# Jensen-Shannon divergence on one core: products by plain fp16 multiply, their sums on TensorE, first pieces through the hardware queue

## Chip, core and metric

The kernel runs on 1 core of a Trainium2 chip. The metric is the device time of one execution in microseconds, the median of three runs. One execution is also taken by the profiler; its rows are what this document reads.

## What is computed

`p` and `q` are 1024 x 4096 in fp32. For every row one number comes out, half the sum of two divergences from the mean of the two rows:

```python
m = 0.5 * (p + q)
kl_pm = np.sum(p * np.log(p / (m + 1e-8) + 1e-8), axis=-1)
kl_qm = np.sum(q * np.log(q / (m + 1e-8) + 1e-8), axis=-1)
return (0.5 * (kl_pm + kl_qm)).astype(np.float32)
```

The kernel takes the quotients apart: it sums `p ln p + q ln q` and subtracts `(p + q) ln m`. The factor `SHIFT` inside the logarithms cancels out between the two.

## The kernel before

The 1024 rows are 8 row groups `g` of 128 partitions. A row group's 4096 columns are cut into pieces of 2048 columns, the first group into 1024, 1024, 2048: 17 pieces in all. For each piece:

- Two DMAs on GpSimd's software queue (lines 75, 76) bring `p` and `q` into one fp16 tile `pq`, of twice the piece's width. The DMA casts from fp32.
- The sum `p + q` is `sps`. For the first three pieces VectorE adds (line 81, `DVE_ADD`), for the others TensorE multiplies blocks of 512 columns by an identity `ident` and adds the two in PSUM (lines 88 and 95).
- ScalarE takes the logarithm of all of `pq` into `ab` (line 105, up to 4096 elements) and of `sps` into `c` (line 114).
- VectorE multiplies `pq` by `ab` and sums along the row in one instruction (line 134, `tensor_tensor_reduce`, which the profile calls CUSTOM_DVE_ANT_0), and does the same with `sps` and `c` (line 144). In the three pieces of `ACT_RED` (8, 11 and 14) it only multiplies (line 123), and ScalarE sums with a `Copy` activation (line 126).

The partial sums are columns of `dacc`; at the end of a row group VectorE adds them into a column of `res` (line 156), and at the very end SyncE stores `res` (line 163). Every engine works through its own instructions in order and waits for the others by semaphores; the framework sets the order of the instructions and when a buffer of a pool is free. `pq` and `ab` have 8 buffers each, `sps` has 2 of 2048 fp32 columns in PSUM. The loads run ahead as far as buffers and the software queue's eight semaphores allow.

Of the kernel before, what the change touches and what calls it, by code (L numbers as in the profile page):

```python
# [1 line left out]

# [5 lines left out]

SHIFT = 6634.0
MMN = 512


@with_exitstack
def kernel(
    ctx: ExitStack,
    tc: tile.TileContext,
    p: bass.AP,  # L20
    q: bass.AP,
    out: bass.AP,
):
    nc = tc.nc
    P = nc.NUM_PARTITIONS

    n_rows, n_cols = p.shape
    assert q.shape == (n_rows, n_cols)
    assert n_rows % P == 0
    n_rg = n_rows // P  # L30

    fp32 = mybir.dt.float32
    fp16 = mybir.dt.float16

    pv = p.rearrange("(p g) d -> g p d", g=n_rg)
    qv = q.rearrange("(p g) d -> g p d", g=n_rg)
    ov = out.rearrange("(p g) -> p g", g=n_rg)

    W = 2048
    assert n_cols == 4096  # L40
    widths = {0: [1024, 1024, 2048]}
    default_w = [W] * (n_cols // W)
    max_terms = 2 * max(len(widths.get(g, default_w)) for g in range(n_rg))

    big = ctx.enter_context(tc.tile_pool(name="big", bufs=8))
    mid = ctx.enter_context(tc.tile_pool(name="mid", bufs=8))
    small = ctx.enter_context(tc.tile_pool(name="small", bufs=1))
    accp = ctx.enter_context(tc.tile_pool(name="accp", bufs=6))
    psp = ctx.enter_context(tc.tile_pool(name="psp", bufs=2, space=bass.MemoryType.PSUM))

    tiny_t = small.tile([P, 1], fp32, tag="tiny")
    nc.vector.memset(tiny_t, 1e-30)  # L52
    epsc_t = small.tile([P, 1], fp32, tag="epsc")
    nc.vector.memset(epsc_t, SHIFT * 1e-8)
    res = small.tile([P, n_rg], fp32, tag="res")
    ident = small.tile([P, P], fp16, tag="ident")
    make_identity(nc, ident)

    nchunks = sum(len(widths.get(g, default_w)) for g in range(n_rg))
    DVE_ADD = {0, 1, 2}  # L60
    ACT_RED = {8, 11, 14}
    idx = 0

    for g in range(n_rg):
        ws = widths.get(g, default_w)
        nt = 2 * len(ws)
        dacc = accp.tile([P, max_terms], fp32, tag="dacc")
        col = 0
        for ci, w in enumerate(ws):
            csl = slice(col, col + w)  # L70
            col += w
            pq = big.tile([P, 2 * w], fp16, tag="pq")
            p0 = pq[:, :w]
            p1 = pq[:, w : 2 * w]
            nc.gpsimd.dma_start(out=p0, in_=pv[g, :, csl])  # L75
            nc.gpsimd.dma_start(out=p1, in_=qv[g, :, csl])  # L76
            pqf = pq[:, : 2 * w]

            if idx in DVE_ADD:
                sps = mid.tile([P, w], fp16, tag="s")  # L80
                nc.vector.tensor_tensor(  # L81
                    out=sps, in0=p0, in1=p1, op=mybir.AluOpType.add
                )
            else:
                sps = psp.tile([P, w], fp32, tag="sps")
                for k in range(w // MMN):
                    blk = slice(k * MMN, (k + 1) * MMN)
                    nc.tensor.matmul(  # L88
                        out=sps[:, blk],
                        lhsT=ident,  # L90
                        rhs=p0[:, blk],
                        start=True,
                        stop=False,
                    )
                    nc.tensor.matmul(  # L95
                        out=sps[:, blk],
                        lhsT=ident,
                        rhs=p1[:, blk],
                        start=False,
                        stop=True,  # L100
                    )

            ab = big.tile([P, 2 * w], fp16, tag="ab")
            abf = ab[:, : 2 * w]
            nc.scalar.activation(  # L105
                out=abf,
                in_=pqf,
                func=mybir.ActivationFunctionType.Ln,
                bias=tiny_t,
                scale=SHIFT,  # L110
            )

            c = mid.tile([P, w], fp16, tag="c")
            nc.scalar.activation(  # L114
                out=c,
                in_=sps,
                func=mybir.ActivationFunctionType.Ln,
                bias=epsc_t,
                scale=SHIFT * 0.5,
            )  # L120

            if idx in ACT_RED:
                nc.vector.tensor_tensor(  # L123
                    out=abf, in0=pqf, in1=abf, op=mybir.AluOpType.mult
                )
                nc.scalar.activation(  # L126
                    out=abf,
                    in_=abf,
                    func=mybir.ActivationFunctionType.Copy,
                    scale=0.5,  # L130
                    accum_out=dacc[:, 2 * ci : 2 * ci + 1],
                )
            else:
                nc.vector.tensor_tensor_reduce(  # L134
                    out=abf,
                    in0=pqf,
                    in1=abf,
                    scale=0.5,
                    scalar=0.0,
                    op0=mybir.AluOpType.mult,  # L140
                    op1=mybir.AluOpType.add,
                    accum_out=dacc[:, 2 * ci : 2 * ci + 1],
                )
            nc.vector.tensor_tensor_reduce(  # L144
                out=c,
                in0=sps,
                in1=c,
                scale=-0.5,
                scalar=0.0,
                op0=mybir.AluOpType.mult,  # L150
                op1=mybir.AluOpType.add,
                accum_out=dacc[:, 2 * ci + 1 : 2 * ci + 2],
            )
            idx += 1

        nc.vector.tensor_reduce(  # L156
            out=res[:, g : g + 1],
            in_=dacc[:, :nt],
            axis=mybir.AxisListType.X,
            op=mybir.AluOpType.add,  # L160
        )

    nc.sync.dma_start(out=ov, in_=res)


# [1 line left out]
_INS = ['p', 'q']  # L167
_OUTS = [((1024,), 'float32')]


# [23 lines left out]
```

## Time and profile before

| What | Before |
|---|---|
| time, median of 3 runs (lowest to highest) | 118.71 us (118.48 to 118.87) |
| span of the profiled execution | 117.0 us |
| VectorE busy | 102.2 us |
| ScalarE busy | 100.2 us |
| TensorE busy with matmuls, mean granted clock | 44.5 us, 0.719 of full |
| GpSimd busy (issuing loads) | 18.8 us |
| DMA busy | from about 3 to 83 us |

The span runs from the first to the last instruction of the profiled execution; the time of a run also holds what lies around it, here 1.7 us more at the median. An engine's busy time is an average over the span. The order of events, and so what the time hangs on, is read from the chain of waits and from each engine's timeline.

### The profile page before, as it was taken

Reading aid. Unit: us, or ns where it says so; the run is one execution under the profiler, and the core shown is the slowest. Engines: PE = TensorE matmul, PEld = TensorE weight load, DVE = VectorE, ACT = ScalarE, POOL = GpSimd, SP = SyncE. Lnnn points to the kernel's source line nnn. Section 1 sums busy time; section 2 is a strip of 40 time slices with the busy share of each in tenths; the row PEclk is TensorE's granted clock in tenths of the full one; section 3 lists DMA queues with packets and bytes.
Section 4 is the critical chain, followed back from the end, with each engine's and each line's share of the span. In section 5 each row is a group of like instructions: output and inputs, shape, how many; then the busy total and the mean of one; then the engine's idle time right before and its main releaser. Section 6 shows DMA issues by size and latency. Waiting matters only on the chain.

```text
span 117.0 us, 477 instructions
## 1 busy us (share of the span) xinstructions
PE 44.5 (38%) x112; PEld 14.8 (13%) x112; DVE 102.2 (87%) x78; ACT 100.2 (86%) x41; POOL 18.8 (16%) x40
## 2 busy tenths in 40 slices
PE   0000001952065381908367900394064393029000
PEld 0000000320021120303021300131021131002000
DVE  0023999989999999999999999999999799996991
ACT  0039976999999999999999999999999999998600
POOL 6943111131111311113211100000000000000000
PEclk9999999999755555555555587559958769955555
DMA  2999999999999999999999999999300000000000
GB/s 10 166 157 206 218 209 220 209 217 209 218 209 217 211 214 213 213 216 211 214 211 216 210 218 207 218 209 220 71 6 0 0 0 0 0 0 0 0 0 1
DMA packets 5042, 16.81 MB, mean 144 GB/s; under 512 B 688, under 2 KB 688, under 8 KB 5040
## 3 DMA queue, kind: packets, MB, share of 16 engines
q0 software_dynamic: 4896, 16.78, 72.8%
q1 hardware_dynamic: 144, 0.00, 0.1%
q8 instruction: 1, 0.02, 0.1%
q14 instruction: 1, 0.01, 0.0%
HBM read 33.55 MB, written 0.00 MB: 287 GB/s over the span
## 4 chain that ended last, share of the span: by engine, by line
ACT 62%; issue 13%; DMA 13%; DVE 6%; POOL 4%; POOLq 0%; ACTq 0%
ACT ab L105 34%; ACT c L114 21%; DMA pq<-in_q_dram 13%; ACT ab L126 8%; DVE ab L134 4%; DVE c L144 2%; POOL pq L75 2%; POOL pq L76 1%; POOL ident masks.py:199 0%; POOL ident masks.py:197 0%; DVE res L156 0%; POOLq masks.py:199 0%; DVE dacc L144 0%; ACTq L105 0%; POOLq L178 0%
## 5 line engine op out<-in xcount | busy, mean ns | idle before, releaser
L105 ACT ACTIVATE ab<-pq,tiny_t 128x4096 f16<-128x4096 f16 (+1 forms) x17 | 59.4, 3513 | 1.9 <-DMA pq<-in_q_dram 1.9
L134 DVE CUSTOM_DVE_ANT_0 ab<-pq,ab 128x4096 f16<-128x4096 f16 (+1 forms) x14 | 57.5, 4115 | 1.7 <-ACT ab L105 1.6
L88 PE MATMUL sps<-pq,ident 128*128 128x512 f16 x56 | 32.0, 571 | 60.4 <-DVE dacc L144 42.4
L144 DVE CUSTOM_DVE_ANT_0 c<-sps,c 128x2048 f16<-128x2048 f32 (+2 forms) x17 | 36.5, 2159 | 0.8 <-ACT c L114 0.8
L95 PE MATMUL sps<-pq,ident 128*128 128x512 f16 x56 | 31.8, 568 | 3.2 <-DMA pq<-in_q_dram 3.2
L114 ACT ACTIVATE c<-sps,epsc_t 128x2048 f16<-128x2048 f32 (+2 forms) x17 | 31.6, 1874 | 0.3 <-PE sps L95 0.3
L95 PEld LDWEIGHTS <-ident 128*128 128x128 f16 x56 | 7.3, 130 | 71.7 <-issue 70.6
L75 POOL DMA_DIRECT2D pq<-in_p_dram x17 | 9.3, 546 | 25.0 <-DMA pq<-in_p_dram 15.9
L76 POOL DMA_DIRECT2D pq<-in_q_dram x17 | 9.1, 538 | 21.1 <-DMA pq<-in_q_dram 21.1
L126 ACT ACTIVATE ab<-ab 128x4096 f16<-128x4096 f16 x3 | 10.9, 3635 | 0.0
L81 DVE TENSOR_TENSOR sps<-pq 128x1024 f16<-128x1024 f16 (+1 forms) x3 | 2.6, 867 | 9.1 <-DMA pq<-in_q_dram 9.1
L88 PEld LDWEIGHTS <-ident 128*128 128x128 f16 x56 | 7.5, 134 | 20.7 <-issue 15.8
L105 ACT ACT_TABLE_LOAD x1 | 1.3, 1283 | 7.6 <-DMA pq<-in_q_dram 7.6
L123 DVE TENSOR_TENSOR ab<-pq,ab 128x4096 f16<-128x4096 f16 x3 | 6.9, 2285 | 0.0
L144 DVE DVE_READ_ACCUMULATOR2_ANT dacc<- 128x1 f32 x17 | 1.4, 82 | 0.0
L156 DVE TENSOR_REDUCE res<-dacc 128x1 f32<-128x4 f32 (+1 forms) x8 | 1.2, 152 | 0.0
L134 DVE DVE_READ_ACCUMULATOR2_ANT dacc<- 128x1 f32 x14 | 1.1, 82 | 0.0
L52 DVE MEMSET tiny_t<- 128x1 f32 x1 | 0.1, 59 | 0.8 <-PEq L178 0.8
L126 ACT ACTIVATION_READ_ACCUMULATOR ab<-ab 128x1 f32 x3 | 0.7, 221 | 0.0
masks.py:199 POOL TENSOR_SCALAR_AFFINE_SELECT ident<-ident 128x128 f16<-128x128 f16 x1 | 0.3, 307 | 0.1
masks.py:197 POOL MEMSET ident<- 128x128 f16 x1 | 0.2, 205 | 0.3 <-POOLq L178 0.3
L178 POOL MEMSET const-float32-0.0<- 128x1 f32 x1 | 0.1, 99 | 0.2 <-issue 0.2
(4 smaller groups left out, 0.4 us busy)
## 6 DMA issues: line engine op xcount, KB each, us to landing
pq<-in_p_dram POOLq DMA_DIRECT2D x15, 512.0 KB, 19.1
pq<-in_q_dram POOLq DMA_DIRECT2D x15, 512.0 KB, 19.4
pq<-in_p_dram POOLq DMA_DIRECT2D x2, 256.0 KB, 5.1
pq<-in_q_dram POOLq DMA_DIRECT2D x2, 256.0 KB, 6.3
out_dram<-res SPq DMA_DIRECT2D x1, 4.0 KB, 1.4
```

Of the source, the lines that this page charges most:

```text
L75: nc.gpsimd.dma_start(out=p0, in_=pv[g, :, csl])
L76: nc.gpsimd.dma_start(out=p1, in_=qv[g, :, csl])
L81: nc.vector.tensor_tensor(out=sps, in0=p0, in1=p1, op=mybir.AluOpType.add)
L88: nc.tensor.matmul(out=sps[:, blk], lhsT=ident, rhs=p0[:, blk], start=True, stop=False,)
L95: nc.tensor.matmul(out=sps[:, blk], lhsT=ident, rhs=p1[:, blk], start=False, stop=True,)
L105: nc.scalar.activation(out=abf, in_=pqf, func=mybir.ActivationFunctionType.Ln, bias=tiny_t, scale=SHIFT,)
L114: nc.scalar.activation(out=c, in_=sps, func=mybir.ActivationFunctionType.Ln, bias=epsc_t, scale=SHIFT * 0.5,)
L123: nc.vector.tensor_tensor(out=abf, in0=pqf, in1=abf, op=mybir.AluOpType.mult)
L126: nc.scalar.activation(out=abf, in_=abf, func=mybir.ActivationFunctionType.Copy, scale=0.5, accum_out=dacc[:, 2 * ci : 2 * ci + 1],)
L134: nc.vector.tensor_tensor_reduce(out=abf, in0=pqf, in1=abf, scale=0.5, scalar=0.0, op0=mybir.AluOpType.mult, op1=mybir.AluOpType.add, accu ...
L144: nc.vector.tensor_tensor_reduce(out=c, in0=sps, in1=c, scale=-0.5, scalar=0.0, op0=mybir.AluOpType.mult, op1=mybir.AluOpType.add, accum_o ...
L156: nc.vector.tensor_reduce(out=res[:, g : g + 1], in_=dacc[:, :nt], axis=mybir.AxisListType.X, op=mybir.AluOpType.add,)
```

## The change

- **Pieces.** Row group 0 is cut into 256, 768, 1024 and 2048 columns, the last group into 2048, 1024, 768 and 256, the others stay at two times 2048: 20 pieces, numbered 0 to 19.
- **First loads.** Pieces 0 and 1 come as fp32 through SyncE's hardware queue (lines 76, 77), the others as before through GpSimd's, now lines 80 and 81. Their sums `s` are added by VectorE in fp32 (line 144).
- **Logarithms.** `ab` is as before (line 163). The sum is now in PSUM tiles `s` of 1024 columns, three buffers, so `c` is taken in halves (line 173). A one-element logarithm on constants stands at the start (line 63). There is no `Copy` activation any more.
- **Products of p and q.** For pieces of at least 1024 columns, VectorE only multiplies (line 165). TensorE sums: it multiplies blocks of 512 columns of `ab` by `half`, an identity times 0.5, and adds all of a row group's blocks up in one 512-column PSUM tile `acc` (line 108). VectorE reduces `acc` to one column (line 116). These matmuls are written behind the sums of the following piece. Smaller pieces keep the multiplying and summing instruction (line 167).
- **Products of the mean** keep it too, in halves (line 176).

The core of the diff:

```diff
-    DVE_ADD = {0, 1, 2}
-    ACT_RED = {8, 11, 14}
+    widths = {0: [256, 768, 1024, 2048], n_rg - 1: [2048, 1024, 768, 256]}
+    HW = 2
-    mid = ctx.enter_context(tc.tile_pool(name="mid", bufs=8))
+    mid = ctx.enter_context(tc.tile_pool(name="mid", bufs=4))
-    psp = ctx.enter_context(tc.tile_pool(name="psp", bufs=2, space=bass.MemoryType.PSUM))
+    psp = ctx.enter_context(tc.tile_pool(name="psp", bufs=3, space=bass.MemoryType.PSUM))
+    psa = ctx.enter_context(tc.tile_pool(name="psa", bufs=2, space=bass.MemoryType.PSUM))
+        if i < HW:
+            t = small.tile([P, 2 * w], fp32, tag=f"pq32_{i}")
+            nc.sync.dma_start(out=t[:, :w], in_=pv[g, :, csl])
+            nc.sync.dma_start(out=t[:, w : 2 * w], in_=qv[g, :, csl])
+    def reduce_on_pe(i, ab):
+        n = 2 * w // MMN
+        for k in range(n):
+            nc.tensor.matmul(
+                out=acc,
+                lhsT=half,
+                rhs=ab[:, k * MMN : (k + 1) * MMN],
+                start=(i == ones[0] and k == 0),
+                stop=(i == ones[-1] and k == n - 1),
+            )
+        if i == ones[-1]:
+            nc.vector.tensor_reduce(
+                out=slot(g), in_=acc, axis=mybir.AxisListType.X, op=Alu.add
+            )
+        if on_pe:
+            nc.vector.tensor_tensor(out=ab, in0=pq, in1=ab, op=Alu.mult)
+        else:
+            nc.vector.tensor_tensor_reduce(
+                out=ab, in0=pq, in1=ab, scale=0.5, scalar=0.0,
+                op0=Alu.mult, op1=Alu.add, accum_out=slot(g),
+            )
+        for o, n, s in sums:
+            c = mid.tile([P, SW], fp16, tag="c")
+            nc.scalar.activation(
+                out=c[:, :n], in_=s[:, :n], func=Act.Ln, bias=epsc_t, scale=SHIFT * 0.5
+            )
```

Below is how instructions stand in a row on an engine, before and after. The names are those of the tiles above; `t` is the new name of `pq`.

ScalarE in the middle of the program, before, around one `Copy` activation:

```order
L105 ACTIVATE ab<-pq,tiny_t 128x4096 [waits DMASW3_49,DMASW2_49]
L114 ACTIVATE c<-sps,epsc_t 128x2048 [waits PE_49]
L126 ACTIVATE ab,dacc<-ab 128x4096 [waits DVE_49]
L114 ACTIVATE c<-sps,epsc_t 128x2048 [waits PE_49]
L105 ACTIVATE ab<-pq,tiny_t 128x4096 [waits DMASW5_49,DMASW4_49]
```

and after:

```order
L173 ACTIVATE c<-s,epsc_t 128x1024 [waits DVE_49,PE_49] x2
L163 ACTIVATE ab<-t,tiny_t 128x4096 [waits DMASW3_49,DMASW2_49]
L173 ACTIVATE c<-s,epsc_t 128x1024 [waits DVE_49,PE_49] x2
L163 ACTIVATE ab<-t,tiny_t 128x4096 [waits DMASW5_49,DMASW4_49]
L173 ACTIVATE c<-s,epsc_t 128x1024 [waits DVE_49,PE_49] x2
```

The activation on `ab` that waited for VectorE is gone; one logarithm of 4096 and two of 1024 alternate.

VectorE in the middle of the program, before, where two products follow each other and a plain multiply comes in between:

```order
L134 ISA ab,dacc<-pq,ab 128x4096 [waits DMASW5_49,DMASW4_49,Activation_49]
L134 ISA dacc 128x1
L156 TENSOR_REDUCE res<-dacc 128x1 [waits DVE_49,Activation_49]
L144 ISA c,dacc<-sps,c 128x2048 [waits Activation_49]
L144 ISA dacc 128x1
L144 ISA c,dacc<-sps,c 128x2048 [waits Activation_49]
L144 ISA dacc 128x1
L123 TENSOR_TENSOR ab<-pq,ab 128x4096 [waits DMASW7_49,DMASW6_49]
```

and after, the whole of one row group's second piece with what follows:

```order
L165 TENSOR_TENSOR ab<-t,ab 128x4096 [waits DMASW3_49,DMASW2_49,Activation_49]
L176 ISA c,dacc<-s,c 128x1024 [waits Activation_49]
L176 ISA dacc 128x1
L176 ISA c,dacc<-s,c 128x1024 [waits Activation_49]
L176 ISA dacc 128x1
L116 TENSOR_REDUCE dacc<-acc 128x1 [waits PE_49]
L165 TENSOR_TENSOR ab<-t,ab 128x4096 [waits DMASW5_49,DMASW4_49,Activation_49]
```

The plain multiply now stands in every full piece; the product with the mean comes in two halves, and the reduction of TensorE's sum once in a row group.

VectorE at the end of the program, after:

```order
L167 ISA ab,dacc<-t,ab 128x1536 [waits DMASW1_49,DMASW0_49,Activation_49]
L167 ISA dacc 128x1
L176 ISA c,dacc<-s,c 128x768 [waits Activation_49]
L176 ISA dacc 128x1
L116 TENSOR_REDUCE dacc<-acc 128x1 [waits PE_49]
L167 ISA ab,dacc<-t,ab 128x512 [waits DMASW3_49,DMASW2_49,Activation_49]
L167 ISA dacc 128x1
L176 ISA c,dacc<-s,c 128x256 [waits Activation_49]
L176 ISA dacc 128x1
L122 TENSOR_REDUCE res<-dacc 128x1 [waits DVE_49]
```

Before, the end was one 4096-element product, one of 2048 and the reduction.

## Rows read from the trace of the kernel before

**Rows 1.** The page, busy time, share of the span and instructions of each engine.

```profile
PE 44.5 (38%) x112; PEld 14.8 (13%) x112; DVE 102.2 (87%) x78; ACT 100.2 (86%) x41; POOL 18.8 (16%) x40
```

**Rows 2.** The page, chain that ended last: shares of the span by engine.

```profile
ACT 62%; issue 13%; DMA 13%; DVE 6%; POOL 4%; POOLq 0%; ACTq 0%
```

**Rows 3.** ScalarE's timeline: start, length (us), line, operation, out<-in, count [idle before].

```profile
10.82 1.13 ACT L114 ACTIVATE c<-sps,epsc_t 128x1024 f16<-128x1024 f16 x1
11.86 1.99 ACT L105 ACTIVATE ab<-pq,tiny_t 128x2048 f16<-128x2048 f16 x1
13.75 1.13 ACT L114 ACTIVATE c<-sps,epsc_t 128x1024 f16<-128x1024 f16 x1
15.62 3.71 ACT L105 ACTIVATE ab<-pq,tiny_t 128x4096 f16<-128x4096 f16 x1 [0.74 <-DMA pq<-in_q_dram]
20.52 3.71 ACT L105 ACTIVATE ab<-pq,tiny_t 128x4096 f16<-128x4096 f16 x1 [1.19 <-DMA pq<-in_q_dram]
...
53.27 3.71 ACT L105 ACTIVATE ab<-pq,tiny_t 128x4096 f16<-128x4096 f16 x1
56.87 1.97 ACT L114 ACTIVATE c<-sps,epsc_t 128x2048 f16<-128x2048 f32 x1
58.72 7.31 ACT L105 ACTIVATE ab<-pq,tiny_t 128x4096 f16<-128x4096 f16 x2
```

**Rows 4.** VectorE's timeline, an early stretch and the end.

```profile
13.53 1.22 DVE L144 CUSTOM_DVE_ANT_0 c<-sps,c 128x1024 f16<-128x1024 f16 x1
...
14.67 2.29 DVE L134 CUSTOM_DVE_ANT_0 ab<-pq,ab 128x2048 f16<-128x2048 f16 x1
...
95.62 2.28 DVE L123 TENSOR_TENSOR ab<-pq,ab 128x4096 f16<-128x4096 f16 x1
97.82 4.42 DVE L134 CUSTOM_DVE_ANT_0 ab<-pq,ab 128x4096 f16<-128x4096 f16 x1
...
102.17 2.29 DVE L144 CUSTOM_DVE_ANT_0 c<-sps,c 128x2048 f16<-128x2048 f32 x1
...
107.84 4.43 DVE L134 CUSTOM_DVE_ANT_0 ab<-pq,ab 128x4096 f16<-128x4096 f16 x1 [1.10 <-ACT ab L105]
...
112.19 2.29 DVE L144 CUSTOM_DVE_ANT_0 c<-sps,c 128x2048 f16<-128x2048 f32 x1
...
114.52 0.16 DVE L156 TENSOR_REDUCE res<-dacc 128x1 f32<-128x4 f32 x1
```

**Rows 5.** Groups by form: busy us, mean ns | idle before.

```profile
L126 ACT ACTIVATE ab<-ab 128x4096 f16<-128x4096 f16 x3 | 10.9, 3635 | 0.0
...
L123 DVE TENSOR_TENSOR ab<-pq,ab 128x4096 f16<-128x4096 f16 x3 | 6.9, 2285 | 0.0
```

**Rows 6.** TensorE's timeline: matmuls around changes of the clock.

```profile
25.41 0.38 PE L95 MATMUL sps<-pq,ident 128*128 128x512 f16 x1 [1.38 <-DMA pq<-in_q_dram]
...
74.97 0.59 PE L88 MATMUL sps<-pq,ident 128*128 128x512 f16 x1 [7.39 <-DVE dacc L144]
...
78.34 0.46 PE L88 MATMUL sps<-pq,ident 128*128 128x512 f16 x1
78.64 0.38 PE L95 MATMUL sps<-pq,ident 128*128 128x512 f16 x1
...
79.93 0.38 PE L95 MATMUL sps<-pq,ident 128*128 128x512 f16 x1
...
92.56 0.59 PE L88 MATMUL sps<-pq,ident 128*128 128x512 f16 x1 [3.34 <-DVE dacc L144]
```

**Rows 7.** Busy time by stretch; behind POOL: granted clock, DMA share, GB/s written.

```profile
30.00:60.00 30.00, 14.69 (x34) 4.66 (x34) 30.00 (x24) 30.00 (x12) 6.36 (x12) 0.51 1.06 213
...
93.00:95.00 2.00, 2.00 (x6) 0.70 (x5) 1.66 (x1) 2.00 (x2) 0.00 (x0) 0.50 0.00 0
```

**Rows 8.** DMA: one stretch of the same view, and the store on SyncE's queue.

```profile
7.00:20.00 13.00, 0.58 (x1) 0.10 (x1) 9.87 (x12) 10.96 (x6) 3.19 (x6) 1.00 1.07 208
out_dram<-res SPq DMA_DIRECT2D x1, 4.0 KB, 1.4
```

More of the change, by code (lines that the diff above doesn't have):

```diff
@@ L54 @@
     nc.vector.memset(epsc_t, SHIFT * 1e-8)
+    warm = small.tile([P, 1], fp32, tag="warm")
+    nc.scalar.activation(out=warm, in_=tiny_t, func=Act.Ln, bias=tiny_t, scale=1.0)
     res = small.tile([P, n_rg], fp32, tag="res")
     ident = small.tile([P, P], fp16, tag="ident")
-    make_identity(nc, ident)
-    nchunks = sum(len(widths.get(g, default_w)) for g in range(n_rg))
-    DVE_ADD = {0, 1, 2}
-    ACT_RED = {8, 11, 14}
[L62 to L104, printed above, removed]
-            nc.scalar.activation(
[L106 to L110, printed above, removed]
-            )
[L113 to L119, printed above, removed]
-            )
[L122 to L161, printed above, removed]
@@ new lines, with load @@
+    half = small.tile([P, P], fp16, tag="half")
+    MAXT = 16
+    state = {}
+    def load(i):
+        g, c0, w, _ = pieces[i]
+        csl = slice(c0, c0 + w)
+        if i < HW:
[3 more added lines that the diff above has]
+        else:
+            t = big.tile([P, 2 * w], fp16, tag="pq")
+            nc.gpsimd.dma_start(out=t[:, :w], in_=pv[g, :, csl])
+            nc.gpsimd.dma_start(out=t[:, w : 2 * w], in_=qv[g, :, csl])
+        state[i] = t
@@ new lines, with group, slot @@
+    rg = {}
+    def group(g):
+        if g not in rg:
+            dacc = accp.tile([P, MAXT], fp32, tag="dacc")
+            big_ones = [i for i, x in enumerate(pieces) if x[0] == g and x[3]]
+            acc = None
+            if big_ones:
+                acc = psa.tile([P, MMN], fp32, tag="acc")
+            rg[g] = [dacc, 0, acc, big_ones]
+        return rg[g]
+    def slot(g):
+        r = group(g)
+        k = r[1]
+        r[1] += 1
+        assert k < MAXT
+        return r[0][:, k : k + 1]
@@ new lines, in reduce_on_pe @@
+    def reduce_on_pe(i, ab):
+        g, _, w, _ = pieces[i]
+        _, _, acc, ones = group(g)
+        n = 2 * w // MMN
[11 more added lines that the diff above has]
+            )
@@ new lines, in close @@
+    def close(g):
+        dacc, n, _, _ = group(g)
+        nc.vector.tensor_reduce(
+            out=res[:, g : g + 1], in_=dacc[:, :n], axis=mybir.AxisListType.X, op=Alu.add
+        )
+    load(0)
+    load(1)
+    load(2)
+    make_identity(nc, ident)
+    nc.vector.tensor_scalar(out=half, in0=ident, scalar1=0.5, scalar2=None, op0=Alu.mult)
+    for i in range(3, len(pieces)):
+        load(i)
+    pending = None
+    for i, (g, c0, w, on_pe) in enumerate(pieces):
+        pq = state[i]
+        p0 = pq[:, :w]
+        p1 = pq[:, w : 2 * w]
+        sums = []
+        if i < HW:
+            s = small.tile([P, w], fp32, tag=f"s32_{i}")
+            nc.vector.tensor_tensor(out=s, in0=p0, in1=p1, op=Alu.add)
+            sums.append((0, w, s))
+        else:
+            for o in range(0, w, SW):
+                n = min(SW, w - o)
+                s = psp.tile([P, SW], fp32, tag="s")
+                for b in range(0, n, MMN):
+                    m = min(MMN, n - b)
+                    for src, first in ((p0, True), (p1, False)):
+                        nc.tensor.matmul(
+                            out=s[:, b : b + m],
+                            lhsT=ident,
+                            rhs=src[:, o + b : o + b + m],
+                            start=first,
+                            stop=not first,
+                        )
+                sums.append((o, n, s))
+        ab = big.tile([P, 2 * w], fp16, tag="ab")
+        nc.scalar.activation(out=ab, in_=pq, func=Act.Ln, bias=tiny_t, scale=SHIFT)
+        if on_pe:
+            nc.vector.tensor_tensor(out=ab, in0=pq, in1=ab, op=Alu.mult)
+        else:
+            nc.vector.tensor_tensor_reduce(
+                out=ab, in0=pq, in1=ab, scale=0.5, scalar=0.0,
+                op0=Alu.mult, op1=Alu.add, accum_out=slot(g),
+            )
+        for o, n, s in sums:
+            c = mid.tile([P, SW], fp16, tag="c")
+            nc.scalar.activation(
+                out=c[:, :n], in_=s[:, :n], func=Act.Ln, bias=epsc_t, scale=SHIFT * 0.5
+            )
+            nc.vector.tensor_tensor_reduce(
+                out=c[:, :n], in0=s[:, :n], in1=c[:, :n], scale=-0.5, scalar=0.0,
+                op0=Alu.mult, op1=Alu.add, accum_out=slot(g),
+            )
+        if pending is not None:
+            j, t = pending
+            reduce_on_pe(j, t)
+            pending = None
+        if on_pe:
+            pending = (i, ab)
+        if i > 0 and pieces[i - 1][0] != g:
+            close(pieces[i - 1][0])
@@ L163 @@
+    close(pieces[-1][0])
     nc.sync.dma_start(out=ov, in_=res)
```

17 lines of the change are left out of this document (11 added, 6 removed).

## Prediction

> **What bounds the kernel now.** The first view is the page's busy time: VectorE 102.2 us and ScalarE 100.2 us of a 117.0 us span [rows 1], so two engines are nearly full and the reader must find out which one the end hangs on. The chain that ended last answers: 62% of it is ScalarE, mostly the logarithms of lines 105 and 114, and VectorE has 6% [rows 2]. ScalarE's timeline shows why: from 15.62 us it waits for data once more, until 20.52, and then runs without a hole to the last `ab` [rows 3]. So the time is three stretches: 15.62 us until columns 0 to 4095 of the first row group have landed; 92.2 us of ScalarE work up to 107.82; and 9.2 us in which VectorE finishes the last piece and the result is stored [rows 3, 4]. The three `Copy` activations of line 126 are ScalarE work that is no logarithm, 10.9 us [rows 5].
>
> I number the new pieces 0 to 19: widths 256, 768, 1024, 2048 in row group 0, then twelve of 2048, then 2048, 1024, 768, 256. S is the start of `ab` of piece 3, which needs the data that landed at 15.62 before.
>
> **ScalarE's work.** Start to start, a 4096-element logarithm takes 3.60 us (53.27 to 56.87), a 2048-element one from PSUM 1.85 (56.87 to 58.72), a 2048-element one from SBUF 1.89 and a 1024-element one from SBUF 1.04 [rows 3]. That is 0.83 to 0.85 us for each 1024 elements. A 1024-element logarithm from PSUM is not in the trace: 1.85 less 0.85 gives 1.00, the SBUF row gives 1.04; I take 1.02. One full piece then costs 3.60 + 2 x 1.02 = 5.64 us. Up to the end of `ab` of piece 18 there are 14 full pieces (78.96), piece 17 (1.89 + 1.02) and the 1536-element logarithm of piece 18 (1.89 - 0.43 = 1.46): 83.33 us from S, against 92.2 before. By edit: the three copies leave (-10.8, at the pitch of a logarithm of that size); the wait before 20.52 is covered (-1.2), since the next data came 4.90 us later and a piece now takes 5.64; each `c` in two halves adds 2.04 - 1.85 = 0.19, over 14 pieces +2.7; the tapered end adds 2.91 + 1.46 - 3.60 = 0.8; the missing 0.3 is rounding and small waits. The table load that the early one-element logarithm pulls forward is worth nothing here, because S waits for data anyway. Pieces 0 to 2 are about 6 us of ScalarE work inside the same wait.
>
> **VectorE.** A plain fp16 multiply of 4096 elements takes 2.20 us start to start, the multiply with a running sum 4.35 (95.62, 97.82, 102.17) [rows 4]; three such multiplies stand in the kernel now, all at 2285 ns [rows 5]. A 1024-wide `c` product takes 1.14 (13.53 to 14.67). The reduction of a 512-column PSUM sum is new: between the 0.16 of a four-column reduction and the 1.14 of the 1024-wide product; by columns, 1.14 - 0.53 = 0.61, which I take. Two full pieces are 2 x 2.20 + 4 x 1.14 + 0.61 + 0.16 = 9.7 us, beside 11.3 us of ScalarE. VectorE thus stops being level with ScalarE and gets 0.8 us of slack per piece; its order puts the next multiply behind the products of the piece before, which end about 4.5 us after that piece's `ab`, before the next `ab` ends. Cost on the path: nothing in the middle.
>
> **TensorE** gets the sums of nearly all products: 246 matmuls in place of 112, 16 for a full piece. Their price depends on the clock. At the lower level (1.2 GHz) they stand 3.37/8 = 0.42 us apart (74.97 to 78.34), at the full one (2.4 GHz) 0.215 (78.64 to 79.93) [rows 6]: 6.7 or 3.4 us per piece against ScalarE's 5.64. This is the one place where a hidden part could come out. I take the full clock: the clock rose after eight matmuls without a gap, and a TensorE that needs 6.7 us of every 5.64 has no gaps. Once it is fast, its bursts are 3.4 us with about 2.2 us between them (it waits for the next multiply). The rows bracket such a hole: after 1.38 us the matmul at 25.41 was still short, after 3.34 us those from 92.56 were slow again [rows 6, 7]. 2.2 lies nearer to the first. A spell at the lower clock costs at most 1.1 us a piece and is then made up, with about 1 us of lead to eat first: 0 in the sum, up to 1 us in the range.
>
> **The start.** S needs 4 MB read from HBM before and after. Before, all of it went through the software queue, at 208 GB/s written, fp16 [rows 8]; now 1 MB of it comes as fp32 through SyncE's queue, with nothing ahead of it there. I take S = 15.6, as it was. Upwards: if the engines' time went by bytes written, the extra 0.5 MB would add 0.52/0.208 = 2.5 us. Downwards: the 2.1 MB that this is in fp16 need 10.1 us at that rate, and the small store on SyncE's queue lands 1.4 us after its issue [rows 8]; issued at 1 us, that makes 12.5 at the very best. Three quarters of the bytes still come through the software queue, so I put the low end half-way back, at 14.0.
>
> **The tail.** Behind `ab` of piece 18 stand on VectorE its 1536-element product (1.14 + 0.54 = 1.68), `c` of 768 (0.87), the PSUM reduction (0.61), 512 elements (0.61), 256 (0.34), the handover that now takes 0.12 (112.19 to 114.52, less 2.21) and the last reduction 0.16: 4.39 us. ScalarE is done 1.8 us after that `ab`, so VectorE ends last. From there to the span's end it is 117.0 - (114.52 + 0.16) = 2.32 us, as now [rows 4]. Together 6.7, against 9.2.
>
> **Sum.** 15.62 + 83.33 + 4.39 + 2.32 = 105.7 us of span, against 117.0. The median of the runs, 118.71, is 1.7 above the profiled span; I keep that: 107.4 us. A difference under 0.3% cannot be told from no change.
>
> **Rivals.**
> First, the hardware pieces come late. SyncE's queue shares 16 engines with the software queue, whose rows are 4 and 8 KB against 1 and 3 KB. If the engines alternate row by row, the small rows get about a quarter of 428 GB/s (2 MB in 4.90 us [rows 3]): 1 MB in 9.8 us, piece 1 at about 12. ScalarE must go in order, and pieces 1 and 2 cost 1.46 + 0.81 + 1.89 + 1.04 = 5.2, so S = 17.2 and the time is 109.0, up to 111 with the extra bytes. For it: nothing here shows the two queues side by side. Against it: at the start the software queue is slow to fill. The Trainium skill (DMA: Bandwidth & Descriptors, Queues, rings and completion order) says that each engine takes turns between queues packet by packet, which speaks for this rival; no run so far shows it.
>
> Second, the clock goes up and down. If half of the pieces fall to the lower level and each keeps its 1.1 us, that is up to 8 us: 110 to 115. Against it: the mean demand, 5.1 us a piece, would still fit, so the waits should be made up. The Trainium skill (TensorE: Matmul & The Clock Gate, A second HAM failure mode: psum-queue depth-cycling) tells of kernels whose small holes between groups on alternating PSUM banks make the clock swing; in this trace it swings, but with holes over 3 us.
>
> Third, slower: the clock stays low throughout. It was at 0.51 of full from 30 to 60 us, through bursts of eight matmuls [rows 7]. Then 240 matmuls' worth behind 15.6 us at 0.421 take 101.0, and 4.2 us of reduction, last piece and store follow: 120.8, time 122.5. TensorE binds from a mean spacing of 5.64/16 = 0.353 us; slower than before begins at (117.0 - 15.6 - 4.2)/240 = 0.405, with over 92% of the matmuls at the low clock. Against it: those bursts were followed by idle stretches, which a TensorE in arrears does not have.
>
> Fourth, the change doesn't do what it says: the multiply runs at the rate of the summing form. Then VectorE needs 2 x (4.35 + 2.28) + 0.77 = 14.0 us for two pieces and binds at 7.0: 15.6 + 3.6 + 98.1 + 3.4 + 4.4 + 2.3 = 127.4, time 129. The three rows of line 123 speak against it.
>
> **How the numbers follow.** The forecast (ScalarE binds, S between 14.0 and 16.8): 0.63, times 105.2 to 108.6; low end from S = 14.0 and 1.00 for the half `c` (30 of them, -0.6). Late hardware pieces: 0.18, 108.6 to 111. Swinging clock: 0.09. Clock low throughout: 0.04. Full-length multiply: 0.02. The remaining 0.04 is something below 105. The range 105.0 to 110.8 holds the first and nearly all of the second, 0.8. Faster by over 0.3%: 0.93, which leaves out the third, the fourth and a sliver of the second; same 0.01; slower 0.06.
>
> **What would show it.** ScalarE: no `Copy`, full pieces 5.64 us apart from S on, halves of `c` at 1.00 to 1.04, no idle time that TensorE or VectorE ended. VectorE: multiplies near 2285 ns, busy about 82 us in all. TensorE: matmuls 0.215 apart in most of the run and a granted clock mostly full. S between 14 and 17. After `ab` of piece 18, 6.7 us to the end. The prediction is wrong if ScalarE waits for a sum `s`, if its 1024-element logarithm from PSUM takes over 1.1 us, if piece 1 lands after 10 us, or if a full piece takes VectorE longer than ScalarE.

## The result, and the profile after

The changed kernel takes 107.36 us (median of four runs) against 118.79 us for the kernel before on the same chip (now four runs, the three of the table ahead and one more): 0.903 of it, 95% interval 0.899 to 0.907. One of the four runs of the changed kernel, 108.3 us, was over 1.5% above the fastest and does not count in that ratio. The prediction said 107.4 us. The sum came out, but several of its terms were off and cancelled each other; this section shows the rows, and the one after the experiments goes through the terms.

The page of the kernel after: busy time, share and instructions of each engine (the row that answers to [rows 1]).

```profile
PE 64.5 (61%) x246; PEld 25.8 (25%) x246; DVE 83.0 (79%) x113; ACT 92.6 (88%) x56; POOL 19.8 (19%) x42
```

VectorE went from 102.2 to 83.0 us, TensorE from 44.5 to 64.5, ScalarE from 100.2 to 92.6. ScalarE is now alone at the top.

ScalarE's timeline, beginning, one full piece, the only hole, and end (answers to [rows 3]; columns as there):

```profile
3.48 0.72 ACT L163 ACTIVATE ab<-t,tiny_t 128x512 f16<-128x512 f32 x1 [1.15 <-DMA t<-in_q_dram]
4.11 0.49 ACT L173 ACTIVATE c<-s,epsc_t 128x256 f16<-128x256 f32 x1
9.56 1.57 ACT L163 ACTIVATE ab<-t,tiny_t 128x1536 f16<-128x1536 f32 x1 [4.96 <-DMA t<-in_q_dram]
11.04 0.92 ACT L173 ACTIVATE c<-s,epsc_t 128x768 f16<-128x768 f32 x1
11.87 1.99 ACT L163 ACTIVATE ab<-t,tiny_t 128x2048 f16<-128x2048 f16 x1
13.76 1.09 ACT L173 ACTIVATE c<-s,epsc_t 128x1024 f16<-128x1024 f32 x1
14.76 3.69 ACT L163 ACTIVATE ab<-t,tiny_t 128x4096 f16<-128x4096 f16 x1
18.36 2.10 ACT L173 ACTIVATE c<-s,epsc_t 128x1024 f16<-128x1024 f32 x2
20.35 3.70 ACT L163 ACTIVATE ab<-t,tiny_t 128x4096 f16<-128x4096 f16 x1
...
74.29 2.27 ACT L173 ACTIVATE c<-s,epsc_t 128x1024 f16<-128x1024 f32 x2
76.45 3.70 ACT L163 ACTIVATE ab<-t,tiny_t 128x4096 f16<-128x4096 f16 x1
...
91.24 2.14 ACT L173 ACTIVATE c<-s,epsc_t 128x1024 f16<-128x1024 f32 x2
93.23 2.03 ACT L163 ACTIVATE ab<-t,tiny_t 128x2048 f16<-128x2048 f16 x1
95.13 1.15 ACT L173 ACTIVATE c<-s,epsc_t 128x1024 f16<-128x1024 f32 x1
96.12 1.61 ACT L163 ACTIVATE ab<-t,tiny_t 128x1536 f16<-128x1536 f16 x1
97.59 0.94 ACT L173 ACTIVATE c<-s,epsc_t 128x768 f16<-128x768 f32 x1
```

Read it from the top. Piece 1, on the hardware queue, is there only at 9.56 us; ScalarE stood still for 4.96 us. From then on it never waits for data: 11.87, 13.76 and 14.76 follow without a hole. So `ab` of piece 3 starts at 14.76 because of piece 1, not because of its own data. Those were there by about 14.1, as GpSimd's timeline shows, where the twelfth load waits until the fourth, `q` of piece 3, has landed:

```profile
14.12 0.53 POOL L81 DMA_DIRECT2D t<-in_q_dram  x1 [1.97 <-DMA t<-in_q_dram]
```

Without the late piece 1 the start could thus have come some 0.65 us earlier in this run, not more. A full piece takes 20.35 - 14.76 = 5.59 us, its two half logarithms 1.99. The one hole is at 74.29: 2.16 to the next `ab` in place of 1.99.

VectorE's timeline at the end (answers to the last three of [rows 4]):

```profile
90.92 0.69 DVE L116 TENSOR_REDUCE dacc<-acc 128x1 f32<-128x512 f32 x1 [0.55 <-PE acc L108]
91.53 2.28 DVE L165 TENSOR_TENSOR ab<-t,ab 128x4096 f16<-128x4096 f16 x1
...
96.09 1.21 DVE L165 TENSOR_TENSOR ab<-t,ab 128x2048 f16<-128x2048 f16 x1
97.22 1.22 DVE L176 CUSTOM_DVE_ANT_0 c<-s,c 128x1024 f16<-128x1024 f32 x1
...
98.36 1.75 DVE L167 CUSTOM_DVE_ANT_0 ab<-t,ab 128x1536 f16<-128x1536 f16 x1
...
102.59 0.16 DVE L122 TENSOR_REDUCE res<-dacc 128x1 f32<-128x8 f32 x1
```

From 91.53 on VectorE has no hole. Its product of piece 18 starts at 98.36, although ScalarE had gone on from `ab` of that piece at 97.59.

TensorE's timeline around two of its holes (answers to [rows 6]):

```profile
37.77 1.46 PE L108 MATMUL acc<-ab,half 128*128 128x512 f16 x6 [2.12 <-DVE ab L165]
...
71.40 2.42 PE L108 MATMUL acc<-ab,half 128*128 128x512 f16 x6 [2.12 <-DVE ab L165]
73.61 1.79 PE L153 MATMUL s<-t,ident 128*128 128x512 f16 x4
```

and busy time by stretch for the same two places (columns as in [rows 7]; the 1.00 and 0.50 ahead of the last two numbers are the granted clock):

```profile
39.00:40.00 1.00, 1.00 (x7) 0.47 (x6) 1.00 (x3) 1.00 (x1) 0.18 (x1) 1.00 1.00 201
...
73.00:74.00 1.00, 1.00 (x3) 0.29 (x2) 0.70 (x3) 1.00 (x1) 0.00 (x0) 0.50 1.07 217
```

Six matmuls after a hole of 2.12 us took 1.46 us in one place and 2.42 in the other, where the clock had dropped to 1.2 GHz. The sums of 73.61 then ended at 75.40, and the second half logarithm of the row at 74.29 would have been due 1.00 us after the first, at 75.29. I read the hole as the wait for these sums; the reading is from the times, since the profile lists no wait there.

### The profile page after: what moved, and what is told of

The parts are those of the page before. It is cut to its first block, busy times and chain, and to the rows that moved or that the text cites. A ratio compares the mean times of both kernels' runs of the same rounds, so it can differ in the third digit from the quotient of the medians.

```text
span 105.1 us, 843 instructions
## 1 busy us (share of the span) xinstructions
PE 64.5 (61%) x246; PEld 25.8 (25%) x246; DVE 83.0 (79%) x113; ACT 92.6 (88%) x56; POOL 19.8 (19%) x42
## 4 chain that ended last, share of the span: by engine, by line
ACT 43%; issue 20%; DMA 17%; DVE 11%; POOL 4%; PE 3%; ACTq 0%; POOLq 0%
ACT ab L163 25%; ACT c L173 18%; DMA t<-in_q_dram 17%; DVE c L176 5%; DVE ab L165 4%; POOL t L80 2%; PE acc L108 2%; POOL t L81 1%; PE s L153 1%; DVE ab L167 1%; DVE dacc L116 1%; POOL ident masks.py:199 0%; POOL ident masks.py:197 0%; DVE res L122 0%; ACTq L173 0%
## 5 line engine op out<-in xcount | busy, mean ns | idle before, releaser
L163 ACT ACTIVATE ab<-t,tiny_t 128x4096 f16<-128x4096 f16 (+5 forms) x20 | 61.1, 3055 | 6.1 <-DMA t<-in_q_dram 6.1
L108 PE MATMUL acc<-ab,half 128*128 128x512 f16 x120 | 34.0, 409 | 24.5 <-DVE ab L165 21.5
L153 PE MATMUL s<-t,ident 128*128 128x512 f16 (+1 forms) x126 | 38.0, 430 | 9.4 <-DMA t<-in_p_dram 7.6
L165 DVE TENSOR_TENSOR ab<-t,ab 128x4096 f16<-128x4096 f16 (+1 forms) x16 | 34.4, 2153 | 7.2 <-ACT ab L163 7.1
L176 DVE CUSTOM_DVE_ANT_0 c<-s,c 128x1024 f16<-128x1024 f32 (+2 forms) x34 | 38.2, 1155 | 0.0
L173 ACT ACTIVATE c<-s,epsc_t 128x1024 f16<-128x1024 f32 (+2 forms) x34 | 35.3, 1097 | 0.0
L108 PEld LDWEIGHTS <-half 128*128 128x128 f16 x120 | 12.3, 102 | 43.5 <-issue 29.1
L80 POOL DMA_DIRECT2D t<-in_p_dram x18 | 9.8, 542 | 29.3 <-DMA t<-in_p_dram 17.6
L81 POOL DMA_DIRECT2D t<-in_q_dram x18 | 9.7, 537 | 25.3 <-DMA t<-in_q_dram 25.3
L116 DVE TENSOR_REDUCE dacc<-acc 128x1 f32<-128x512 f32 x8 | 5.5, 691 | 3.9 <-PE acc L108 3.9
```

Of the source, the lines that this page charges most:

```text
L80: nc.gpsimd.dma_start(out=t[:, :w], in_=pv[g, :, csl])
L81: nc.gpsimd.dma_start(out=t[:, w : 2 * w], in_=qv[g, :, csl])
L108: nc.tensor.matmul(out=acc, lhsT=half, rhs=ab[:, k * MMN : (k + 1) * MMN], start=(i == ones[0] and k == 0), stop=(i == ones[-1] and k == n ...
L116: nc.vector.tensor_reduce(out=slot(g), in_=acc, axis=mybir.AxisListType.X, op=Alu.add)
L153: nc.tensor.matmul(out=s[:, b : b + m], lhsT=ident, rhs=src[:, o + b : o + b + m], start=first, stop=not first,)
L163: nc.scalar.activation(out=ab, in_=pq, func=Act.Ln, bias=tiny_t, scale=SHIFT)
```

## The experiments

The kernel before takes 118.4 to 119.4 us (median) on the chips used, so the ratios to it are compared. The span of a run is on record beside its time, and some comparisons need it.

**All loads through the software queue.** Pieces 0 and 1 come as fp16 on GpSimd's queue:

```diff
-            t = small.tile([P, 2 * w], fp32, tag=f"pq32_{i}")
-            nc.sync.dma_start(out=t[:, :w], in_=pv[g, :, csl])
-            nc.sync.dma_start(out=t[:, w : 2 * w], in_=qv[g, :, csl])
+            t = small.tile([P, 2 * w], fp16, tag=f"pq16_{i}")
+            nc.gpsimd.dma_start(out=t[:, :w], in_=pv[g, :, csl])
+            nc.gpsimd.dma_start(out=t[:, w : 2 * w], in_=qv[g, :, csl])
```

> Pieces 0 and 1 come through the software queue as fp16, all else as in the changed kernel. Theory: the start is limited by the bytes that have to land; in the kernel before, the software queue had the same columns there at 7.62 (1024), 10.71 (2048) and 15.62 us (4096), so ab of piece 3 starts at 15.6 in place of 14.76 and the time is 108.2 us (+0.9). Rival: the hardware pieces are late because the queues share the engines; in order on one queue piece 1 lands by 7.6 in place of 9.56, ab of piece 3 starts at 14.7 or earlier and the time is 107.3 or less.

108.58 us, 0.911 of before (0.906 to 0.917). ScalarE's timeline of this kernel, pieces 1 and 3:

```profile
7.63 1.57 ACT L163 ACTIVATE ab<-t,tiny_t 128x1536 f16<-128x1536 f16 x1 [2.09 <-DMA t<-in_q_dram]
...
16.65 3.71 ACT L163 ACTIVATE ab<-t,tiny_t 128x4096 f16<-128x4096 f16 x1 [1.96 <-DMA t<-in_q_dram]
```

Piece 1 is there 1.9 us sooner, as the rival said, and still piece 3 starts 1.9 us later, since its own data come last. The theory's side holds, by a larger amount in the profiled run (16.65 for the expected 15.6), which was the slowest of the four. In time it is weaker: the interval touches the changed kernel's (0.899 to 0.907). In six profiles with the changed kernel's order of loads piece 3 started at 14.43 to 14.98, so with this cut of the pieces the hardware queue does bring the start forward. The cut matters too, as the next run shows.

**The products alone.** Pieces as before, software queue, no taper:

```diff
-    widths = {0: [256, 768, 1024, 2048], n_rg - 1: [2048, 1024, 768, 256]}
+    widths = {0: [1024, 1024, 2048]}
-    HW = 2
+    HW = 0
+    if pending is not None:
+        j, t = pending
+        reduce_on_pe(j, t)
     close(pieces[-1][0])
```

> Only the products part of the change: plain multiply, sums on TensorE, half-width c; pieces as before (1024, 1024, 2048, then all 2048), all through the software queue, no taper. Theory: ScalarE binds from 15.6 us on, 14 x 5.6 + 3.6 to the end of the last ab, then multiply 2.2, two products 2.28, reduction 0.6, last column 0.16, store 2.3: span 105.3, time 107.4, so the other two parts together are worth less than 1 us. Rival: start and taper carry part of the gain, and without them the time is over 109.5.

109.99 us, 0.920 (0.913 to 0.927). The theory is wrong and the rival holds, though barely: 109.99 is over its 109.5, while the ratio would make 109.3 on the chip of the prediction. Most of the gain is there without the other two parts, but they are worth some 2 us together, not under 1. ScalarE's timeline of this kernel:

```profile
9.69 2.00 ACT L163 ACTIVATE ab<-t,tiny_t 128x2048 f16<-128x2048 f16 x1 [1.21 <-DMA t<-in_q_dram]
14.70 3.71 ACT L163 ACTIVATE ab<-t,tiny_t 128x4096 f16<-128x4096 f16 x1 [3.01 <-DMA t<-in_q_dram]
18.32 1.10 ACT L173 ACTIVATE c<-s,epsc_t 128x1024 f16<-128x1024 f32 x1
...
30.73 3.27 ACT L173 ACTIVATE c<-s,epsc_t 128x1024 f16<-128x1024 f32 x3
...
100.05 2.28 ACT L173 ACTIVATE c<-s,epsc_t 128x1024 f16<-128x1024 f32 x2
```

The big piece starts at 14.70, with all data through the software queue and after a wait for its own. So the start of the run before, 16.65, belongs to its finer cut as well as to the queue; how much to each is open. But no `c` stands ahead of it any more: the framework put the two of the first pieces behind it, so 2.0 us of logarithms moved out of the wait for data and onto the path. To the end of the last `ab` it takes 100.05 - 14.70 = 85.4 us; 15 x 3.60 + 30 x 1.00 = 84.0 are work, the rest small waits. Such a shift in the order is not in the widths or the queues; the diff does not show it, ScalarE's timeline does.

**Multiply and sum on VectorE.** One word, so that no piece takes the plain multiply:

```diff
-            pieces.append((g, col, w, w >= 1024))
+            pieces.append((g, col, w, False))
```

> The changed kernel with the multiply-and-sum instruction of VectorE in every piece, so neither plain multiply nor sums of products on TensorE, and still no Copy on ScalarE. Theory: VectorE then needs 4.35 + 2.28 = 6.63 us for a piece of which ScalarE needs 5.59, and binds: span 18.4 + 14 x 6.63 + 3.4 + 3.8 + 2.3 = 120.7, time 122.8. Rival: the gain is the Copy that left ScalarE, and the time stays at 107 to 109.

123.97 us, 1.042 (1.034 to 1.049), slower than before. Its page:

```profile
PE 53.5 (44%) x126; PEld 17.3 (14%) x126; DVE 109.2 (90%) x121; ACT 93.5 (77%) x56; POOL 19.8 (16%) x42
```

The theory holds. ScalarE lost its `Copy` here as well, and it did not help: VectorE binds with 109.2 us. In these kernels the `Copy` could go because VectorE's product became a plain multiply and TensorE took the sum.

**TensorE's sum twice.** Each block goes through TensorE twice, with 0.25:

```diff
-        for k in range(n):
+        for k in range(2 * n):
-                rhs=ab[:, k * MMN : (k + 1) * MMN],
+                rhs=ab[:, (k // 2) * MMN : (k // 2 + 1) * MMN],
```

> Every block of products is summed twice on TensorE, with 0.25 in place of 0.5: 24 matmuls for a piece in place of 16. Theory: at 0.215 us each that is 5.2 us, still under ScalarE's 5.59, and a TensorE with hardly a hole keeps the full clock: the time stays within 0.5 us of 107.4. Rival: the swinging clock costs; at the lower level a piece needs 10.1 us, each spell of some 3.4 us puts TensorE 1.7 us in arrears with little slack to make it up, and the time is 110 or more.

107.82 us, 0.905 (0.901 to 0.910), the changed kernel's 0.903 within the intervals. Its page and one stretch of busy time:

```profile
PE 84.5 (80%) x366; PEld 36.3 (34%) x366; DVE 83.5 (79%) x113; ACT 92.7 (88%) x56; POOL 19.8 (19%) x42
```

```profile
30.00:60.00 30.00, 28.47 (x129) 12.40 (x127) 26.39 (x31) 30.00 (x18) 6.36 (x12) 1.00 1.06 213
```

20 us more of TensorE work, and ScalarE's 30.00 of 30 us untouched. With hardly a hole the granted clock is 1.00 in this stretch (0.996 over the run, 0.939 in the changed kernel), and the time is no lower for it: a steady clock gave nothing back that can be measured.

**TensorE's sum three times.** The same with `3 * n`, `k // 3` and a sixth:

> Every block of products is summed three times on TensorE, with a sixth in place of a half: 32 matmuls for a piece. Theory: TensorE binds as soon as its spacing times its matmuls exceeds ScalarE's 5.59 us for a piece; 32 x 0.215 = 6.9, so the 14 full pieces take 14 x 1.3 = 18 us longer: span 123, time 125, with a full clock throughout. Rival: waits of TensorE for VectorE, not its own pace, hold the pieces; then the extra matmuls fall partly into holes and the time is under 118.

126.44 us, 1.065 (1.051 to 1.080; two runs). Its timeline by stretch, and who waited for TensorE:

```profile
30.00:60.00 30.00, 30.00 (x141) 13.62 (x139) 24.80 (x27) 30.00 (x16) 6.33 (x12) 1.00 1.06 214
```

```profile
ACT c L173 <- PE s L153: 21.3, 6, 4.8
```

TensorE is full, 141 matmuls in 30 us are 0.213 us apart, and ScalarE waited 21.3 us for sums, near the 18 worked out. So the cover is known from both sides: 24 matmuls a piece are free, 32 are not, and the changed kernel has 16.

**The hardware queue alone at first.** GpSimd's loads wait for piece 1, through two one-element copies on GpSimd into the tile of piece 2:

```diff
             t = big.tile([P, 2 * w], fp16, tag="pq")
+            if i == 2:
+                nc.gpsimd.tensor_copy(out=t[:, 0:1], in_=state[1][:, 1535:1536])
+                nc.gpsimd.tensor_copy(out=t[:, w : w + 1], in_=state[1][:, 1535:1536])
```

> GpSimd's loads of pieces 2 and up wait until piece 1 has landed (two one-element copies on GpSimd read its last column), so that the hardware queue has the DMA engines for itself at first; the first software load is then that of p of piece 3. Theory: piece 1 was late, at 9.56, because the software queue took the larger part; alone, 1 MB at 428 GB/s is there at about 5.3. The bytes in total stay, so ab of piece 3 starts at 14.5 to 15 and the time is 107.4 within 0.6. Rival: the hardware queue is slow by itself with rows of 1 and 3 KB; piece 1 lands after 8 us all the same, and everything behind it 3 us later, 110 us.

110.03 us, 0.921 (0.918 to 0.925). ScalarE's timeline, pieces 1 to 3, and DMA by stretch:

```profile
6.20 1.57 ACT L166 ACTIVATE ab<-t,tiny_t 128x1536 f16<-128x1536 f32 x1 [0.76 <-DMA t<-in_q_dram]
...
14.78 2.00 ACT L166 ACTIVATE ab<-t,tiny_t 128x2048 f16<-128x2048 f16 x1 [6.18 <-DMA t<-in_q_dram]
...
17.68 3.70 ACT L166 ACTIVATE ab<-t,tiny_t 128x4096 f16<-128x4096 f16 x1
```

```profile
6.00:8.00 2.00, 0.00 (x0) 0.00 (x0) 1.27 (x4) 1.80 (x2) 1.83 (x4) 1.00 0.00 0
```

On the cause the theory holds: alone, piece 1 is there at 6.20 in place of 9.56, so in the changed kernel the software queue beside it costs it 3.4 us. On the time it was wrong. It came to the rival's 110 us without the rival's mechanism. The engines moved nothing from 6 to 8 us, while GpSimd first made its two copies (6.17 to 7.16 us) and then issued its first loads, and the big piece started 2.9 us later. I had counted bytes and forgotten the gap that a held-back queue leaves; about 1 us of it is the copies of this edit.

**Alternating queues at the start, and plain multiplies to the end.** Two edits, apart and together:

```diff
-    widths = {0: [256, 768, 1024, 2048], n_rg - 1: [2048, 1024, 768, 256]}
+    widths = {0: [256, 256, 512, 1024, 2048], n_rg - 1: [2048, 1024, 768, 256]}
-    HW = 2
+    HW = {0, 2}
```

```diff
-            pieces.append((g, col, w, w >= 1024))
+            pieces.append((g, col, w, w >= 1024 or g == n_rg - 1))
+    if pending is not None:
+        j, t = pending
+        reduce_on_pe(j, t)
     close(pieces[-1][0])
```

> Row group 0 is cut into 256, 256, 512, 1024, 2048, and the two queues alternate: pieces 0 and 2 by SyncE's hardware queue, 1, 3 and all later ones by the software queue. Theory: ab of the 2048-column piece starts at 14.76 because piece 1 landed on the hardware queue only at 9.56 and ScalarE goes in order; with the work before it fed by both queues in turn only the landing of that piece itself, about 13.9, is left: start 13.9, time 106.5. Rival: the engines' time sets the start whatever the order, and the time stays within 0.3 us of 107.4.

> In the last row group all products go by plain multiply and TensorE, also those of the 768 and 256 columns. Theory: VectorE is the last engine there, it runs without a hole for the last 11 us; the two multiplies cost 0.86 and 0.32 in place of 1.68 and 0.61, so the end comes 1.0 us earlier: time 106.4. Rival: the reduction now has to wait for TensorE's last sum at the very end, which eats the gain: within 0.3 us of 107.4.

> Both of the two edits before: alternating queues at the start and plain multiplies in the last row group. If start and tail add up, 107.4 - 0.9 - 1.0 = 105.5.

Start 107.05 us, 0.898 (0.894 to 0.902); tail 106.54, 0.893 (0.890 to 0.896); both 105.81, 0.887 (0.882 to 0.891). VectorE's end in the kernel with the tail alone:

```profile
98.60 0.95 DVE L165 TENSOR_TENSOR ab<-t,ab 128x1536 f16<-128x1536 f16 x1
...
101.23 0.69 DVE L116 TENSOR_REDUCE dacc<-acc 128x1 f32<-128x512 f32 x1
101.95 0.16 DVE L122 TENSOR_REDUCE res<-dacc 128x1 f32<-128x6 f32 x1
```

The stretch from piece 18's product to the last reduction took 102.59 - 98.36 = 4.23 us in the changed kernel and takes 3.35 here. The start was not settled by this: its interval overlaps the changed kernel's, and the big piece started at 14.79 in its profiled run. The changed kernel and the two with this start therefore went on one chip together:

> The changed kernel itself, unaltered, on the same chip as the next two, since the kernel before takes between 118.4 and 119.4 us on the chips so far. Expected: 0.903 of before, start of ab of piece 3 at 14.7 to 14.8 us.

> The alternating start again. Theory: the hardware pieces set the changed kernel's start, and this order brings the start of the 2048-column piece to about 13.9, 0.9 us (0.7%) less than the changed kernel on the same chip. Rival: the landing of that piece is limited by the bytes and moves with them from run to run, 13.8 to 14.8; then the gain is under 0.4%.

> Alternating start and plain multiplies in the last row group again. Expected 1.6% under the changed kernel on the same chip if both parts hold, 1.0% if only the tail does.

Changed kernel 107.34 us, 0.905 (0.900 to 0.909); start 106.98, 0.902 (0.897 to 0.907); both 106.40, 0.896 (0.891 to 0.900). ScalarE's row of the big piece in the second of these:

```profile
14.12 3.71 ACT L164 ACTIVATE ab<-t,tiny_t 128x4096 f16<-128x4096 f16 x1 [0.88 <-DMA t<-in_q_dram]
```

In the four profiles with this order the piece started at 14.79, 13.82, 14.12 and 14.84, each time after a wait of 0.9 us for its own data. The changed kernel's own start in this group was 14.43, earlier than the 14.7 expected. The rival was right: the start is then limited by the landing of that piece, which moves by 1 us from run to run. The order makes 0.3% in time, within the intervals, and nothing in the span: the median span is 105.2 us in both. The 0.36 us between 107.34 and 106.98 lie outside the span, where a run of the changed kernel has 2.1 us and one with this start 1.8; no run shows why.

The tail is worth 0.58 us on this chip (106.98 to 106.40) and 1.24 us on the one before (107.05 to 105.81); the stretch in the profiles gave 0.88. The version with both is the fastest found, about 1% under the changed kernel on the same chip, which is what was expected if only the tail holds.

## Why the prediction was right, term by term

| Term | Predicted | Measured |
|---|---|---|
| start of `ab` of piece 3 | 15.62 | 14.76 |
| from there to the end of `ab` of piece 18 | 83.33 | 82.83 |
| wait before VectorE takes piece 18 | 0 | 0.77 |
| VectorE from there to the last reduction's end | 4.39 | 4.39 |
| store | 2.32 | 2.35 |
| span | 105.7 | 105.1 |
| around the span | 1.71 | 2.13 |
| time | 107.4 | 107.23 (profiled run), 107.36 (median) |

- **What bounds.** Right: ScalarE, at 5.59 us a piece for the predicted 5.64. The half logarithm from PSUM cost 1.00, the lower of the two ends. That is 0.05 a piece and 0.7 over 14 pieces, less the hole of 0.17. By the letter of its own sign ("wrong if ScalarE waits for a sum `s`") that hole would count against the prediction; at 0.17 us of 105 it changes nothing.
- **VectorE's cover.** Right in the middle of the program: the plain multiplies of 4096 elements all ran at 2286 ns, the reduction of `acc` at 0.61 start to start (90.92 to 91.53), and VectorE's busy time is 83.0 for the predicted 82. The run with the multiply-and-sum shows what the cover was worth: 1.042 against 0.903 of before, some 16.5 us.
- **TensorE's cover.** Right, and now bounded on both sides by the runs with double and triple sums. My reason for the full clock was thin: it rose after eight matmuls without a gap at 78.34, but between 33 and 67 us of the kernel before six bursts of eight had stayed slow. What held is that TensorE then ran from 15.28 to 24.5 us without a hole, and from 20.89 on its matmuls stood 0.215 us apart, at the full clock. The clock did swing, as the second rival had it: after seven holes of 2.1 us it fell three times. That went with one ScalarE hole of 0.17 us, not with the 8 us of the rival; the run with double sums, with hardly a swing, was no faster. The Trainium skill (TensorE: Matmul & The Clock Gate, A second HAM failure mode: psum-queue depth-cycling) tells of a kernel whose clock swings because TensorE idles briefly between groups of matmuls, and which loses throughput by it. The trace agrees on the swing; the loss is there on TensorE (2.42 us for six matmuls in place of 1.46) and does not reach the end.
- **The start.** The step that failed in its reasoning, mis-sized by 0.86 us. I kept 15.62 as if the queue made no difference. It made two: the hardware queue brought the data of piece 3 forward (there by 14.1, against 16.65 with the software queue alone and the same pieces, though 14.70 with coarser ones), and the first rival's mechanism, hardware pieces delayed by the software queue, was at work: piece 1 at 9.56, against 6.20 alone. The rival had 12. The sum 9.56 + 1.48 + 0.83 + 1.89 + 1.00 = 14.76 is its working, with a smaller first term. The Trainium skill (DMA: Bandwidth & Descriptors, Queues, rings and completion order) says that engines take turns between queues; the 3.4 us agree with it, but no run here shows in what portions.
- **The tail.** The 4.39 us were right to the hundredth and yet incomplete. I took VectorE to be free when `ab` of piece 18 ended. It was 0.77 late: the multiply of the last full piece began 0.29 late behind the reduction of `acc`, which had waited 0.55 for TensorE, and from there VectorE had 98.36 - 91.53 = 6.83 us of work, ScalarE 97.59 - 91.24 = 6.35. So ScalarE got through the short pieces while VectorE was still busy with the last long one. The run with plain multiplies to the end took 0.88 us off that stretch, and the time fell by 0.6 to 1.2.
- **Around the span.** I set the median of the runs against a span that was not the median's. A run's time stands 2.1 us above its own span in the changed kernel, and a run of before with 118.38 us had a span of 116.2. The 1.71 was too small by 0.4. The distance is not the same for every kernel: it is 2.1 to 2.2 us too with double or triple sums or with the tail alone, but 1.7 to 1.9 in all runs with the multiply-and-sum, the held-back queue, the alternating start, or all loads of the finer pieces through the software queue. What sets it stays open.

So the sum held by -0.86 - 0.50 + 0.77 + 0.03 + 0.42 = -0.14 us. That it came so close is luck: nothing ties the early start to the late tail or to the time around the span. Each of the errors was a tenth of the gain or less; the gain itself, ScalarE freed of its copies with VectorE and TensorE both under cover, came as worked out.

## What to carry to other kernels

When two engines are level, an operation leaves the one only if the other is relieved in the same change: with the cheaper product on VectorE, taking the copies off ScalarE went with 9 us of gain (109.99 against 119.1), and without it the kernel was slower than before. A tapered end, of smaller and smaller pieces, helps only if the engine that comes last also gets through them sooner: sum that engine's work from its last full piece on, not from the last small one. And take the distance between time and span from one and the same run; before a small difference in time is put down to a change, see whether the span shows it.

## What the runs showed of the hardware that was not expected

- A load on SyncE's queue is slower beside loads on GpSimd's: 1 MB on the hardware queue was there at 9.56 us beside the software queue and at 6.20 alone.
- A software queue that is held back leaves a gap: the last bytes of the hardware queue moved before 6 us, `ab` of piece 1 started at 6.2, and the first bytes of the software queue moved after 8.5 us.
- The same hole of 2.1 us in TensorE's work was followed by the full clock in four places and by the half clock in three (after 26.62, 60.19 and 71.40 us); in the kernel with the tail alone a hole of 1.64 us was followed by the half clock too.
